# One transformer layer on one core: a unit's weight sums placed between its remainders on VectorE, and raw weight blocks laid side by side

## The chip, the core and the metric

The kernel runs on one core of a Trainium2 chip. The metric is the device time of one execution, in microseconds (us). The core has engines that run beside each other, each with its own queue of instructions in order: TensorE (PE in the profile; PEld is its weight load) multiplies matrices, VectorE (DVE) and ScalarE (ACT) work on elements, GpSimd (POOL) does small work and issues some of the transfers, and SyncE (SP) issues most of them. Transfers between the main memory and the on-chip memory run on 16 DMA engines. Results of TensorE lie in eight banks of accumulators until VectorE or ScalarE reads them. Engines wait for each other through semaphores.

## The reference

One layer over 512 tokens of 2048 features, in float32. Cut to what matters here:

```python
h = rmsnorm(x, norm_mix)
qa, ka, va, qb, kb, vb, ga, gb = split(h @ w_in)
out_a = window_attention(...); out_b = neighbourhood_attention(...)
x = x + (sigmoid(ga) * (out_a @ w_branch_a) + sigmoid(gb) * (out_b @ w_branch_b)) @ w_out
u = rmsnorm(x, norm_ffn) @ w_up                      # 2048 -> 11264
u = centred depthwise convolution of width 3 over the tokens, plus conv_b
gate, val = split(u)
x = x + (silu(gate) * val) @ w_down                  # 5632 -> 2048
```

The gates ga and gb, the up projection and the down projection are the products that the change touches.

## The kernel before

**Float32 by halves.** Each operand of a matmul is split in two: a rounded part, hi (wh for weights), and the remainder, lo (wl). A product is three matmuls: hi by hi, hi by lo, lo by hi. ScalarE rounds (a cast), VectorE subtracts (the remainder).

**Seven products for eight.** Most of the gates and of the two feed-forward projections are computed in 2 x 2 blocks with seven block products where eight would be usual. A `Product` unit is a block of 256 x 512 weights: two blocks of 128 rows (b = 0, 1) by two halves of 256 columns (h = 0, 1). Three of the four raw blocks are used as they are, and four weight forms are sums: with f the unit's tile of seven slices of 128 x 256, `load` (line 588) brings the raw blocks into slices 0, 1, 2 and 6 and `sums` (line 597) makes slices 3 to 6, the first instruction (line 600) two of them at once from the fourth raw block, the second (603) and the third (604) each from the result of the one before. On the activations' side `form_sums` (line 668) does the same kind of work, and `combine` (line 784) puts the seven results of a finished block together in three parts, `one`, `two` and `three`, which read the banks and so free them.

**Units kept.** Some units' weights are made early: `fetch` (line 606) brings the raw blocks by GpSimd's queue, `add` (line 617) makes the sums on VectorE, `store` writes them to main memory (`kept`), in stages where VectorE has room. For such a unit (`made`) `load` brings three raw blocks and the four kept slices, and `sums` does nothing. Of each block of the up projection units 2, 3 and 7 of eight are kept, of the first such block all; of the down projection only a few.

**Forms.** `prep` (line 632) makes the rounded parts and remainders of a unit in two groups: slices 0 to 3 (tag a) and slices 4 to 6 (tag b): a cast on ScalarE (line 645), then a subtraction on VectorE (line 646), for each group. The weight tiles are double buffered by the unit's parity, so a cast waits until TensorE has finished with the unit two before.

**The order.** The loop of `products` (line 690) issues 42 matmuls of a unit (seven forms, two halves of columns, three matmuls each), then calls `advance` (line 179). `advance` first calls `prep` of the unit after next; at the end of a block the parts of `combine` go in as `between`: the first ahead of group a, the second ahead of group b, the third behind. Then it calls `sums` of the unit one further and `load` of the unit two further than that, and last the early work. Behind `advance`, the loop runs one queued piece of work (activation, convolution) and the caller's `after`, which near the changes of stage splits activations that have just been loaded (`split_act`: casts at line 1075, remainders at line 1076). `keep` holds instructions in the order in which the program issues them; the matmuls are placed by the scheduler. The tile f has four buffers, so the load of a unit waits for the remainder of group b four units before; SP issues these loads in order, line 75.

**Stages.** Attention and its projections until about 600 us; gates, branches and w_out to about 1180; the up projection in 22 blocks of eight units to about 2005; then the down projection in three parts of pairs (7, 7 and 8) by four blocks of columns. Three of these twelve blocks (`PLAIN`, the first of part 0 and the last of parts 0 and 1) use plain tiles without sums (`tiles_by_halves`, casts at line 746, remainders at 747). The 195 units that make their sums on the spot are spread over the gates, the up projection and the down projection.

Of the kernel before, what the change touches and what calls it, by code (L numbers as in the profile page):

```python
# [18 lines left out]
P = 128  # L19
# [20 lines left out]
def trunk_kernel(  # L40
# [95 lines left out]
    class Plain:  # L136
# [18 lines left out]
        def prep(self, *between, pieces=1):  # L155
            self.load(pieces)
            for work in between:
                work()
            hi = wst["p"].tile([P, 1024], F32R, tag="hi", name="hi", bufs=2)
            lo = wst["p"].tile([P, 1024], F32R, tag="lo", name="lo", bufs=2)  # L160
            n = 1024 // pieces
            for c in range(0, 1024, n):
                nc.scalar.copy(hi[:, c:c + n], self.raw[:, c:c + n])  # L163
                nc.vector.tensor_tensor(  # L164
                    lo[:, c:c + n], self.raw[:, c:c + n], hi[:, c:c + n].bitcast(F32),
                    ALU.subtract)
            self.hi = hi.rearrange("p (a n) -> p a n", a=self.kpb)
            self.lo = lo.rearrange("p (a n) -> p a n", a=self.kpb)

    def prep_to(n, between=(), **kw):  # L170

        for u in units[at["prep"]:n + 1]:
            if getattr(u, "first", -1) > ffn.get("limit", -1):
                break
            u.prep(*between, **kw)
            between = ()
            at["prep"] += 1
        for work in between:
            work()
# [394 lines left out]
    class Product:  # L574
# [13 lines left out]
        def load(self):  # L588
            f = self.f = ffn["f"].tile([P, 7, 256], F32, tag="f", name="f", bufs=4)
            dma(f[:, 0:2], self.w[:, :, 0])  # L590
            dma(f[:, 2], self.w[:, 1, 1])
            if self.made:
                dma(f[:, 3:], self.kept)
            else:
                dma(f[:, 6], self.w[:, 0, 1])

        def sums(self):
            if not self.made:
                f = self.f
                keep(nc.vector.tensor_tensor(  # L600
                    f[:, 3:5], f[:, 2::-2], f[:, 6].unsqueeze(1).to_broadcast([P, 2, 256]),
                    ALU.add))
                keep(nc.vector.tensor_tensor(f[:, 5], f[:, 4], f[:, 2], ALU.add))  # L603
                keep(nc.vector.tensor_tensor(f[:, 6], f[:, 5], f[:, 1], ALU.add))

        def fetch(self):

            if "q" in ffn:
                x = quad("u").rearrange("p m (t n) -> p (m t) n", t=2)
                self.early = x[:, :2], x[:, 2:]  # L610
            else:
                self.early = [slot().rearrange("p (t n) -> p t n", t=2) for _ in range(2)]
# [19 lines left out]
        def prep(self, *between):  # L632
            self.parts = []
            for b, (tag, n) in enumerate((("a", 4), ("b", 3))):
                if between:
                    between[b]()
# [10 lines left out]
                self.parts += [(hi[:, i], lo[:, i]) for i in range(n)]  # L647
            for work in between[2:]:
                work()
# [72 lines left out]
    class Tiles:  # L722
# [13 lines left out]
        def sums(self):  # L736
            pass

        def prep(self, *between):
# [9 lines left out]
            for work in between:  # L749
                work()  # L750
# [488 lines left out]
```

## Time and profile before

| what | value |
|---|---|
| median of 3 runs | 2465.93 us (2465.27 to 2466.05) |
| profiled execution, from its first instruction to its last | 2464.1 us |
| TensorE busy | 2436.6 us, 99% of the span |
| VectorE busy | 1899.6 us, 77% |
| ScalarE busy | 1283.5 us, 52% |
| moved by DMA | 525.45 MB, 213 GB/s on average |
| mean granted TensorE clock | 0.998 |

The profile is of one execution, and gives its span; the runs' time holds some 1.8 us more, what lies around the span. A busy share is an average over stages: TensorE at 99% can still wait in a stage, and an engine at 77% can be the one that it waits for there. In the lists of instructions, `out<-in` names the tiles that an instruction writes and reads, `xcount` how many there are, and square brackets the idle time of the engine ahead of the instruction and what ended it.

### The profile page before, as it was taken

To read this page: it belongs to the slowest core of one execution; us is meant where nothing else is said; L and a number is where in the kernel's file an instruction comes from. 1 tells how busy PE (TensorE), PEld (TensorE's weight loads), DVE (VectorE), ACT (ScalarE), POOL (GpSimd) and SP (SyncE) were. 2 spreads that over 40 slices of the span, in tenths; PEclk is the share of its full clock that TensorE was granted. 3 is DMA by queue.
4 is the path that set the end of the run, shared out by engine and by line. 5 is a ranking of instruction groups with operands and counts; after the bars stand their busy time and mean duration, and the time that the engine had idled before them with its cause. 6 is when DMAs were issued, how large, how long until landed. Compare 5 with 4: busy or idle time off the path is not lost.

```text
span 2464.1 us, 45745 instructions
## 1 busy us (share of the span) xinstructions
PE 2436.6 (99%) x17430; PEld 2276.2 (92%) x17430; DVE 1899.6 (77%) x3003; ACT 1283.5 (52%) x1962; POOL 330.5 (13%) x406
## 2 busy tenths in 40 slices
PE   9999999999999999999999999999999999999998
PEld 7888888888999888888999999999999999999998
DVE  6787667655888656557888888888888878696898
ACT  5354554365644322334666666666666666453633
POOL 1322122301000111111011111110111101000000
PEclk9999999999999999999999999999999999999999
DMA  5766766746655677777588888888888897766754
GB/s 197 257 230 213 234 207 230 238 139 205 197 163 175 200 271 245 237 232 245 166 213 230 224 225 224 218 234 222 224 228 218 234 277 187 218 187 176 221 158 131
DMA packets 340700, 525.45 MB, mean 213 GB/s; under 512 B 30720, under 2 KB 234112, under 8 KB 340480
## 3 DMA queue, kind: packets, MB, share of 16 engines
q1 hardware_dynamic: 254656, 319.68, 41.8%
q0 software_dynamic: 48384, 128.91, 21.8%
q10 hardware_dynamic: 37440, 73.94, 7.8%
q8 instruction: 136, 2.23, 0.4%
q14 instruction: 84, 0.69, 0.1%
HBM read 377.80 MB, written 98.57 MB: 193 GB/s over the span
## 4 chain that ended last, share of the span: by engine, by line
PE 94%; DVE 2%; DMA 1%; ACT 1%; issue 1%; SPq 0%; DVEq 0%; ACTq 0%
PE mm L78 91%; PE tr L78 2%; PE tr L503 1%; PE tr L351 0%; DVE wl L646 0%; DVE s L1076 0%; DMA a<-in_x_t 0%; DMA s<-act 0%; DMA f<-in_w_down 0%; ACT wh L645 0%; DVE u L795 0%; DVE s L687 0%; ACT s L1075 0%; DMA sums<-s 0%; DVE s L620 0%
## 5 line engine op out<-in xcount | busy, mean ns | idle before, releaser
L78 PE MATMUL mm<-s,wh 128*128 128x256 f32 (+1 forms) x9620 | 1725.0, 289 | 6.6 <-ACT wh L645 2.5
L78 PEld LDWEIGHTS mm<-s,wh 128*128 128x128 f32 x9620 | 1437.1, 188 | 48.7 <-ACT wh L645 3.1
L78 PE MATMUL mm<-s,wl 128*128 128x256 f32 (+1 forms) x4810 | 1249.9, 289 | 3.5 <-DVE wl L646 3.5
L78 PEld LDWEIGHTS mm<-s,wl 128*128 128x128 f32 x4810 | 851.0, 188 | 24.7 <-DVE wl L646 4.5
L645 ACT CAST wh<-f 128x1024 fp32r<-128x1024 f32 (+1 forms) x566 | 516.9, 942 | 482.5 <-PE mm L78 331.3
L646 DVE TENSOR_TENSOR wl<-f,wh 128x1024 fp32r<-128x1024 f32 (+1 forms) x566 | 601.8, 1088 | 147.7 <-ACT wh L645 146.3
L78 PE MATMUL mm<-hi,s 128*128 128x512 f32 x896 | 284.9, 394 | 5.7 <-ACT hi L163 5.7
L747 DVE TENSOR_TENSOR wl<-f,wh 128x1024 fp32r<-128x1024 f32 x85 | 104.1, 1224 | 165.4 <-ACT wh L746 159.7
L746 ACT CAST wh<-f 128x1024 fp32r<-128x1024 f32 x85 | 89.4, 1052 | 238.8 <-PE mm L78 207.0
L78 PEld LDWEIGHTS mm<-hi,s 128*128 128x128 f32 x896 | 167.6, 189 | 38.4 <-ACT hi L163 5.7
L163 ACT CAST hi<-raw 128x1024 fp32r<-128x1024 f32 (+1 forms) x97 | 100.9, 1040 | 188.5 <-PE mm L78 153.9
L78 PE MATMUL mm<-s,hi 128*128 128x512 f32 x640 | 195.4, 392 | 2.1 <-ACT o L519 1.6
L164 DVE TENSOR_TENSOR lo<-raw,hi 128x1024 fp32r<-128x1024 f32 (+1 forms) x97 | 117.5, 1211 | 102.8 <-ACT hi L163 98.7
L78 PE MATMUL mm<-lo,s 128*128 128x512 f32 x448 | 176.3, 395 | 0.0
L78 PEld LDWEIGHTS mm<-s,hi 128*128 128x128 f32 x640 | 119.2, 188 | 25.9 <-ACT o L519 1.8
L600 DVE TENSOR_TENSOR f<-f 128x512 f32<-128x512 f32 x195 | 133.5, 685 | 0.0
L1045 POOL DMA_DIRECT2D o<-a x44 | 52.9, 1202 | 557.8 <-ACT a L1044 336.9
L78 PE MATMUL mm<-s,lo 128*128 128x512 f32 x320 | 118.8, 391 | 0.0
L620 DVE TENSOR_TENSOR s<-s 128x256 f32<-128x256 f32 x236 | 93.2, 419 | 17.1 <-DMA s<-in_w_up 15.0
L78 PEld LDWEIGHTS mm<-lo,s 128*128 128x128 f32 x448 | 84.4, 188 | 16.6
L1042 ACT ACTIVATE o<-u,smalls 128x512 f32<-128x512 f32 x88 | 71.2, 809 | 33.3 <-DVE t L677 30.1
L603 DVE TENSOR_TENSOR f<-f 128x256 f32<-128x256 f32 x195 | 83.0, 426 | 6.7
(150 smaller groups left out, 2029.5 us busy)
## 6 DMA issues: line engine op xcount, KB each, us to landing
f<-sums SPq DMA_DIRECT2D x88, 512.0 KB, 5.3
f<-in_w_up SPq DMA_DIRECT2D x176, 256.0 KB, 3.8
o<-a POOLq DMA_DIRECT2D x88, 511.0 KB, 7.4
f<-in_w_up SPq DMA_DIRECT2D x281, 128.0 KB, 3.8
raw<-in_w_in SPq DMA_DIRECT2D x63, 512.0 KB, 4.4
sums<-s ACTq DMA_DIRECT2D x118, 256.0 KB, 4.1
s<-in_w_up POOLq DMA_DIRECT2D x86, 256.0 KB, 5.4
s<-act SPq DMA_DIRECT2D x168, 128.0 KB, 4.2
```

What stands on the lines that cost most here:

```text
L78: return nc.tensor.matmul(o, l, r, start=start, stop=stop, skip_group_check=True).ins
L163: nc.scalar.copy(hi[:, c:c + n], self.raw[:, c:c + n])
L164: nc.vector.tensor_tensor(lo[:, c:c + n], self.raw[:, c:c + n], hi[:, c:c + n].bitcast(F32), ALU.subtract)
L600: keep(nc.vector.tensor_tensor(f[:, 3:5], f[:, 2::-2], f[:, 6].unsqueeze(1).to_broadcast([P, 2, 256]), ALU.add))
L603: keep(nc.vector.tensor_tensor(f[:, 5], f[:, 4], f[:, 2], ALU.add))
L620: add = lambda *args: keep(nc.vector.tensor_tensor(*args, ALU.add))
L645: keep(nc.scalar.copy(hi, f))
L646: keep(nc.vector.tensor_tensor(lo, f, hi.bitcast(F32), ALU.subtract))
L746: keep(nc.scalar.copy(hi, self.f))
L747: keep(nc.vector.tensor_tensor(lo, self.f, hi.bitcast(F32), ALU.subtract))
L1042: keep(nc.scalar.activation(self.o[:, m], u[:, m], AF.Identity, bias=cb[:, i:i + 1], scale=cw[:, i, 1:2]))
L1045: keep(nc.gpsimd.dma_start(self.o[:, :, 1:], first[:, :, :S - 1], accum_op=ALU.add))
```

## The change

It does three things. The raw blocks get other slices: w[:, 1] (the second block of rows, both halves of columns) goes to slices 0 and 1, w[:, 0] to slices 2 and 3; slice 3 is overwritten by a sum. So a unit with sums has two loads in place of three, and where the two halves of columns adjoin in memory (w_in, w_down) a row of a load is 2 KB in place of 1 KB. `prep` puts the forms back in the old order for the matmuls. `fetch` and `add` follow the same layout.

The three instructions of `sums` become a list. `advance` hands them to `prep` as hooks: the first goes between group a and group b of the unit that is being prepared, behind group a's remainder; the second goes behind group b; the third is carried to the next `advance` and stands ahead of group a there. The parts of `combine` stand in the same three places, each behind the sum that is there. The sums still belong to the unit one further than the one prepared.

```diff
     def advance(*between):
-        prep_to(at["use"] + 1, between)
-        for phase, d in (("sums", 2), ("load", 4)):
+        def phase_units(phase, d):
             while at[phase] < len(products_) and products_[at[phase]].ready(phase, at["use"] + d):
-                getattr(products_[at[phase]], phase)()
                 at[phase] += 1
+                yield products_[at[phase] - 1]
+
+        hooks = [[*carried], [], []]
+        carried.clear()
+        for u in phase_units("sums", 2):
+            run_all(carried)
+            carried.clear()
+            ops = u.sums()
+            for place, op in zip((1, 2), ops):
+                hooks[place].append(op)
+            carried.extend(ops[2:])
+        for place, op in enumerate(between):
+            hooks[place].append(op)
+        prep_to(at["use"] + 1, hooks)
+        for u in phase_units("load", 4):
+            u.load()
         make_early()
...
         def load(self):
             f = self.f = ffn["f"].tile([P, 7, 256], F32, tag="f", name="f", bufs=4)
-            dma(f[:, 0:2], self.w[:, :, 0])
-            dma(f[:, 2], self.w[:, 1, 1])
+            dma(f[:, 0:2], self.w[:, 1])
             if self.made:
+                dma(f[:, 2], self.w[:, 0, 0])
                 dma(f[:, 3:], self.kept)
             else:
-                dma(f[:, 6], self.w[:, 0, 1])
+                dma(f[:, 2:4], self.w[:, 0])
 
         def sums(self):
-            if not self.made:
-                f = self.f
-                keep(nc.vector.tensor_tensor(
-                    f[:, 3:5], f[:, 2::-2], f[:, 6].unsqueeze(1).to_broadcast([P, 2, 256]),
-                    ALU.add))
-                keep(nc.vector.tensor_tensor(f[:, 5], f[:, 4], f[:, 2], ALU.add))
-                keep(nc.vector.tensor_tensor(f[:, 6], f[:, 5], f[:, 1], ALU.add))
+            if self.made:
+                return []
+            f = self.f
+            add = lambda *args: keep(nc.vector.tensor_tensor(*args, ALU.add))
+            return [
+                lambda: add(f[:, 4:2:-1], f[:, 2:0:-1],
+                            f[:, 3].unsqueeze(1).to_broadcast([P, 2, 256])),
+                lambda: add(f[:, 5], f[:, 4], f[:, 1]),
+                lambda: add(f[:, 6], f[:, 5], f[:, 0])]
 
         def fetch(self):
...
-            for h, x in enumerate(self.early):
-                keep(nc.gpsimd.dma_start(x, self.w[:, :, h]))
+            for b, x in enumerate(self.early):
+                keep(nc.gpsimd.dma_start(x, self.w[:, b]))
 
         def add(self):
             a, b = self.early
...
-            add(c[:, 0], b[:, 1], b[:, 0])
-            add(c[:, 1], a[:, 0], b[:, 0])
-            add(b[:, 0], c[:, 1], b[:, 1])
-            add(b[:, 1], b[:, 0], a[:, 1])
-            self.early = c, b
+            add(c[:, 1], a[:, 0], a[:, 1])
+            add(c[:, 0], b[:, 1], a[:, 1])
+            add(a[:, 0], c[:, 1], b[:, 1])
+            add(a[:, 1], a[:, 0], b[:, 0])
+            self.early = c, a
...
-        def prep(self, *between):
-            self.parts = []
+        def prep(self, *hooks):
+            forms = []
             for b, (tag, n) in enumerate((("a", 4), ("b", 3))):
-                if between:
-                    between[b]()
+                run_all(hooks[b])
...
                 f = self.f[:, 4 * b:4 * b + n]
                 keep(nc.scalar.copy(hi, f))
                 keep(nc.vector.tensor_tensor(lo, f, hi.bitcast(F32), ALU.subtract))
-                self.parts += [(hi[:, i], lo[:, i]) for i in range(n)]
-            for work in between[2:]:
-                work()
+                forms += [(hi[:, i], lo[:, i]) for i in range(n)]
+            run_all(*hooks[2:])
+            self.parts = [forms[i] for i in (2, 0, 1, 3, 4, 5, 6)]
```

`run_all` calls the pieces of work in the lists it is given. Plain units and tiles have no sums; they call the hooks as before.

More of the change, by code (lines that the diff above doesn't have):

```diff
@@ L153, in load, with prep @@
                 c0 += n
-        def prep(self, *between, pieces=1):
+        def prep(self, *hooks, pieces=1):
             self.load(pieces)
-            for work in between:
-                work()
+            run_all(*hooks)
             hi = wst["p"].tile([P, 1024], F32R, tag="hi", name="hi", bufs=2)
@@ L168, in prep, with prep_to @@
             self.lo = lo.rearrange("p (a n) -> p a n", a=self.kpb)
-    def prep_to(n, between=(), **kw):
+    def prep_to(n, hooks=((), (), ()), **kw):
         for u in units[at["prep"]:n + 1]:
@@ L174, in prep_to, with run_all @@
                 break
-            u.prep(*between, **kw)
-            between = ()
+            u.prep(*hooks, **kw)
+            hooks = (), (), ()
             at["prep"] += 1
-        for work in between:
-            work()
+        run_all(*hooks)
+    def run_all(*hooks):
+        for works in hooks:
+            for work in works:
+                work()
+    carried = []
     def advance(*between):
-        prep_to(at["use"] + 1, between)
-        for phase, d in (("sums", 2), ("load", 4)):
+        def phase_units(phase, d):
             while at[phase] < len(products_) and products_[at[phase]].ready(phase, at["use"] + d):
-                getattr(products_[at[phase]], phase)()
                 at[phase] += 1
+                yield products_[at[phase] - 1]
[13 more added lines that the diff above has]
+            u.load()
         make_early()
@@ L589, in load @@
             f = self.f = ffn["f"].tile([P, 7, 256], F32, tag="f", name="f", bufs=4)
-            dma(f[:, 0:2], self.w[:, :, 0])
-            dma(f[:, 2], self.w[:, 1, 1])
+            dma(f[:, 0:2], self.w[:, 1])
             if self.made:
+                dma(f[:, 2], self.w[:, 0, 0])
                 dma(f[:, 3:], self.kept)
             else:
-                dma(f[:, 6], self.w[:, 0, 1])
+                dma(f[:, 2:4], self.w[:, 0])
         def sums(self):
-            if not self.made:
-                f = self.f
-                keep(nc.vector.tensor_tensor(
-                    f[:, 3:5], f[:, 2::-2], f[:, 6].unsqueeze(1).to_broadcast([P, 2, 256]),
-                    ALU.add))
-                keep(nc.vector.tensor_tensor(f[:, 5], f[:, 4], f[:, 2], ALU.add))
-                keep(nc.vector.tensor_tensor(f[:, 6], f[:, 5], f[:, 1], ALU.add))
+            if self.made:
[7 more added lines that the diff above has]
+                lambda: add(f[:, 6], f[:, 5], f[:, 0])]
         def fetch(self):
             if "q" in ffn:
-                x = quad("u").rearrange("p m (t n) -> p (m t) n", t=2)
-                self.early = x[:, :2], x[:, 2:]
-            else:
-                self.early = [slot().rearrange("p (t n) -> p t n", t=2) for _ in range(2)]
-            for h, x in enumerate(self.early):
-                keep(nc.gpsimd.dma_start(x, self.w[:, :, h]))
+                x = quad("u").rearrange("p b (h n) -> p b h n", h=2)
+                self.early = x[:, 0], x[:, 1]
+            else:
+                self.early = [slot().rearrange("p (h n) -> p h n", h=2) for _ in range(2)]
+            for b, x in enumerate(self.early):
+                keep(nc.gpsimd.dma_start(x, self.w[:, b]))
         def add(self):
@@ L646, in prep @@
                 keep(nc.vector.tensor_tensor(lo, f, hi.bitcast(F32), ALU.subtract))
-                self.parts += [(hi[:, i], lo[:, i]) for i in range(n)]
-            for work in between[2:]:
-                work()
+                forms += [(hi[:, i], lo[:, i]) for i in range(n)]
+            run_all(*hooks[2:])
+            self.parts = [forms[i] for i in (2, 0, 1, 3, 4, 5, 6)]
     def make_early():
@@ L736, in sums, with prep @@
         def sums(self):
-            pass
-        def prep(self, *between):
+            return []
+        def prep(self, *hooks):
             hi, lo = (
@@ L748, in prep @@
             self.hi, self.lo = (v.rearrange("p (b c) n -> p b (c n)", b=2) for v in (hi, lo))
-            for work in between:
-                work()
+            run_all(*hooks)
     class TilesByHalves(Tiles):
```

## The prediction

> **What bounds the kernel now.** I read the page first, then the chain that ended last in order of time, then the busy time by stretches, and last each place where TensorE sat idle.
>
> ```profile
> span 2464.1 us, 45745 instructions
> ...
> PE 2436.6 (99%) x17430; PEld 2276.2 (92%) x17430; DVE 1899.6 (77%) x3003; ACT 1283.5 (52%) x1962; POOL 330.5 (13%) x406
> ```
> ```profile
> 636.33 547.52 PE mm L78 x3286
> ...
> 1202.54 802.51 PE mm L78 x7058
> ```
> TensorE is the bound. From 636 to 2005 us the chain is matmul after matmul, so whatever VectorE or the queues do there is hidden. Most of the changed instructions run there and can earn nothing. Only a stretch in which TensorE waits can pay. The next view has the end of the kernel, the down projection; behind the stretch and its length stand the busy time and the matmuls started on PE, then PEld, DVE, ACT, POOL, the clock, the DMA share and GB/s.
>
> ```profile
> 2004.00:2016.00 12.00, 8.47 (x53) 7.47 (x52) 7.21 (x14) 9.22 (x22) 1.20 (x1) 0.85 1.08 293
> 2016.00:2164.00 148.00, 147.45 (x1281) 146.93 (x1280) 116.44 (x196) 81.75 (x152) 10.00 (x10) 0.99 0.76 216
> 2164.00:2182.00 18.00, 16.85 (x146) 16.52 (x145) 17.51 (x38) 11.66 (x25) 1.72 (x2) 1.00 0.87 229
> 2182.00:2295.00 113.00, 113.00 (x996) 113.00 (x995) 86.87 (x131) 48.32 (x71) 5.16 (x6) 1.00 0.65 181
> 2295.00:2352.00 57.00, 53.41 (x462) 52.62 (x461) 54.04 (x97) 31.85 (x62) 3.93 (x6) 1.00 0.66 187
> ```
> The undisturbed row gives the pace: 996 matmuls in 113 us, 8.81 per us. At that pace 18 us hold 158.7 and 57 us hold 502.4. With 146 and 462 started, the third row lost 12.7 / 8.81 = 1.4 us and the fifth 40.4 / 8.81 = **4.6 us**; in both VectorE is busy 95 to 97%. The first row lost 52.7 / 8.81 = 6.0 us, but VectorE is busy for only 7.2 of 12 us there. The stalls one by one (idle time and its releaser in brackets):
>
> ```profile
> 2181.27 0.39 PE L78 MATMUL mm<-s,wl 128*128 128x256 f32 x1 [1.15 <-DVE wl L646]
> ...
> 2320.69 0.39 PE L78 MATMUL mm<-s,wl 128*128 128x256 f32 x1 [0.60 <-DVE wl L646]
> ...
> 2326.56 0.39 PE L78 MATMUL mm<-s,wl 128*128 128x256 f32 x1 [0.82 <-DVE wl L646]
> ...
> 2345.02 0.38 PE L78 MATMUL mm<-s,wl 128*128 128x256 f32 x1 [0.92 <-DVE wl L646]
> ...
> 2351.60 1.09 PE L78 MATMUL mm<-s,wh 128*128 128x256 f32 x7 [1.25 <-ACT wh L645]
> ```
> Four wait for a remainder (wl, line 646), the fifth for a cast (wh, line 645). They sum to 4.74 us; the count of matmuls says 6.0, since TensorE also restarts slowly. This 6.0 us is what the change can win. What else TensorE idles lies ahead of 636 us, in the stages of the attention, and of the changed code only the fetches and adds run there.
>
> **The sums on VectorE.** One unit with weight sums, in the stretch where line 1076 splits activations too:
>
> ```profile
> 2313.54 2.09 DVE L646 TENSOR_TENSOR wl<-f,wh 128x1024 fp32r<-128x1024 f32 x2
> 2315.54 0.69 DVE L600 TENSOR_TENSOR f<-f 128x512 f32<-128x512 f32 x1
> 2316.27 0.43 DVE L603 TENSOR_TENSOR f<-f 128x256 f32<-128x256 f32 x1
> 2316.73 0.43 DVE L604 TENSOR_TENSOR f<-f 128x256 f32<-128x256 f32 x1
> 2317.07 2.43 DVE L1076 TENSOR_TENSOR s<-s 128x256 fp32r<-128x256 f32 x7
> 2319.42 2.09 DVE L646 TENSOR_TENSOR wl<-f,wh 128x1024 fp32r<-128x1024 f32 x2
> ```
> ```profile
> 2340.62 0.68 DVE L795 TENSOR_TENSOR u<-mm,t 128x512 f32<-128x512 f32 x1
> 2341.22 0.68 DVE L795 TENSOR_TENSOR u<-mm,o 128x512 f32<-128x512 f32 x1
> ```
> The three sums read each other's results, and start 0.73, 0.46 and 0.34 us ahead of the next instruction. Instructions that do not depend on each other overlap: line 795 starts again after 0.60 us at the same 512 elements, and seven splits of 256 take 2.35 us, 0.34 each. So the dependence costs 0.13 + 0.12 = **0.25 us a unit**. The change puts a remainder between the first sum and the second, and carries the third into the next call. Where splits stand between the second and third, all 0.25 us goes; where nothing does, only 0.13. The numbers of instructions and elements stay.
>
> The Trainium skill, "VectorE: DVE Perf Modes", section "The DRAIN you can't avoid", says that the next operation does not start until the pipe is empty, and that chaining without semaphores measured the same time. By it, reordering saves nothing here, and the sum is that of the second rival below. The rows above differ: a sum that needs the one before starts after it ends, a split before the last one ends.
>
> **The cast that waits for a sum.** Behind the splits VectorE catches up:
>
> ```profile
> 2353.59 0.69 DVE L600 TENSOR_TENSOR f<-f 128x512 f32<-128x512 f32 x1
> ...
> 2355.44 2.09 DVE L646 TENSOR_TENSOR wl<-f,wh 128x1024 fp32r<-128x1024 f32 x2 [0.24 <-ACT wh L645]
> 2357.45 0.69 DVE L600 TENSOR_TENSOR f<-f 128x512 f32<-128x512 f32 x1
> ```
> ```profile
> 2354.36 1.79 ACT L645 CAST wh<-f 128x1024 fp32r<-128x1024 f32 x2 [2.07 <-DVE f L600]
> ```
> ScalarE's cast of the first group reads the first sum's result, so it starts when that sum ends (2354.28), and VectorE then waits for it. A unit takes 3.86 us. After the change the first sum stands ahead of the second remainder, most of a unit earlier, and that wait goes: 2.01 (the pair) + 0.60 + 0.46 + 0.34 = 3.41 us, so 0.45 us a unit goes here.
>
> ```profile
> 2308.79 0.96 DVE L646 TENSOR_TENSOR wl<-f,wh 128x768 fp32r<-128x768 f32 x1 [0.83 <-ACT wh L645]
> ...
> 2349.67 0.69 DVE L600 TENSOR_TENSOR f<-f 128x512 f32<-128x512 f32 x1
> ```
> At 2308.79 VectorE idles 0.83 us ahead of a second remainder; the first sum of the next unit, 0.60 us, fits in there.
>
> Against the stalls: in the stretch to 2182 three units save 0.75, and VectorE's idle time there, 18 - 17.51 = 0.49, can go: 1.24 against the stall of 1.15, so I take the whole 1.4. From 2295 units with splits follow each other every 5.88 us (2313.54 to 2319.42). By 2320, four of them and the filled idle make 4 x 0.25 + 0.60 = 1.6, against 0.60; by 2326, 1.85 against 0.60 + 0.82 = 1.42; by 2345, three catch-up units more make 1.85 + 3 x 0.45 = 3.2, against 2.34. The fifth stall stands behind the first sum at 2349.67, itself behind the combination of a finished block; that sum now comes ahead of the block's second part. There VectorE is the limit: 3.2 won and its own idle, some 3.8 of the 4.6. Sum: 1.4 + 3.8 = **5.2 us**.
>
> What is delayed: the second remainder by 0.60 us (the first sum ahead of it), and the combination's middle part, which frees banks, by as much at block ends. Both have a unit's time, 42 matmuls / 8.81 = 4.8 us, except at the ends of blocks; that is why I take 3.8 and not 4.6. A new wait: the cast of the second group needs the third sum, which now follows the splits.
>
> ```profile
> 2307.93 0.83 ACT L645 CAST wh<-f 128x768 fp32r<-128x768 f32 x1 [1.76 <-issue]
> 2308.67 0.71 ACT L1075 CAST s<-s 128x256 fp32r<-128x256 f32 x2
> ```
> Behind that cast on ScalarE stand the casts for the next splits (line 1075), and VectorE's splits wait for those. From the third sum's end VectorE has two remainders, 2.01, and two sums, 0.60 + 0.34, to do first; ScalarE is through the cast and two split casts in 0.83 + 0.71 = 1.54. So I take nothing, and as the other end 0.5 us for each unit with sums and splits, of which the timeline shows four up to 2181 and six from 2295.
>
> **The loads.**
>
> ```profile
> L600 DVE TENSOR_TENSOR f<-f 128x512 f32<-128x512 f32 x195 | 133.5, 685 | 0.0
> ```
> ```profile
> SPq L75 <- DVE wl L646: 844.2, 267, 23.6
> ```
> ```profile
> 2361.50 0.89 SPq L75 DMA_DIRECT2D f<-in_w_down x2
> ```
> The 195 units with sums need two loads where they had three; 0.45 us of SP's time goes with each. SP waits 844 us for remainders to free its buffers, which hides it, so I cost it at nothing, up to 0.45 us where SP is late. Longer rows change the matrices whose blocks adjoin, not the up projection's, which lie apart. Line 600 never waited for a load (0.0 idle), and a load is issued some three units before its sum, so moving that sum up by one remainder adds no wait; without this cover VectorE would stand still, with the remainder, the combination and the splits behind.
>
> ```profile
> DVE s L620 <- DMA s<-in_w_up: 15.0, 9, 3.5
> ```
> ```profile
> 475.00:500.00 25.00, 23.76 (x121) 19.93 (x120) 17.58 (x42) 9.96 (x22) 4.76 (x9) 1.00 0.61 218
> ```
> The sums made early (fetch and add) keep their counts; the first add now needs the first of the two loads, not the second. At nine waits and one add of 0.34 us that is at most 3 us of VectorE's, and TensorE idles but 1.24 us of the 25 around some of them; I take nothing.
>
> **The rivals.**
>
> Second: **only the wait for the cast goes**, because dependent sums cost the same wherever they stand. Then the 0.49 of idle wins 0.4 of the first 1.4, and 0.60 at 2308, 3 x 0.24 and 1.2 of the fifth stall win 2.5 of the second: 2.9 us, 2463.0. For it: in catch-up the second and third sum stay adjacent. Against: the overlap in the rows above.
>
> Third: **the new wait takes it back.** 10 x 0.5 = 5.0 us of VectorE's time against 5.2 won, 2465.7. For it: ScalarE runs one call ahead of VectorE in the splits, and loses that. Against: it is busy for only 11.66 of 18 and 31.85 of 57 us.
>
> Fourth: **the change of stage at 2005 mends too.**
>
> ```profile
> 1995.39 0.40 SPq L75 DMA_DIRECT2D f<-in_w_down  x1
> ```
> ```profile
> 2004.78 1.05 ACT L746 CAST wh<-f 128x1024 fp32r<-128x1024 f32 x1 [4.64 <-DMA f<-in_w_down]
> ```
> ```profile
> 2010.00:2015.00 5.00, 3.11 (x17) 2.92 (x18) 2.59 (x4) 3.50 (x8) 0.00 (x0) 0.74 1.07 264
> 2015.00:2020.00 5.00, 5.00 (x28) 5.00 (x28) 4.69 (x10) 1.45 (x5) 0.00 (x0) 0.58 0.82 272
> ```
> The first tile of w_down is issued at 1995.39 and its cast starts at 2004.78, the DMA engines full (1.07), then the clock falls to 0.58. An earlier load could keep the clock: 28 matmuls instead of 44 in the last row are 1.8 us, and part of the gap before 1 to 2 more: 3 us beside the 5.2, 2457.7. Against: those loads keep their size and order.
>
> Fifth, **slower**: the first sum now writes its two blocks in descending order. Before, it read them so, at 685 ns, and a read cost nothing; such a write the trace does not show. Bounds: nothing, or a second pass, 0.69 us. I take nothing, by the row of the descending read. Above 0.25 us it eats the gain of a unit with splits; at 0.69 the ten such units lose 10 x (0.69 - 0.25) = 4.4 us, and three catch-up units 3 x (0.69 - 0.45) = 0.7, on top of today's stalls: 2471.0.
>
> **How the numbers follow.** The profiled execution spans 2464.1 us, 1.8 less than the median of the runs, 2465.93; I take the 5.2 us off the median: **2460.7**. Chances: this forecast 0.44 (2459.2 to 2462.4), the second 0.22, the third 0.13, the fourth 0.10, the fifth 0.11. A measurement tells 0.2% from no change, 4.9 us, so faster means below 2461.0. Some 0.28 of my forecast's 0.44 lies there, its lower part, and with the fourth that is faster 0.38; the rest of it, the second and the third make same 0.51; slower 0.11. The range is 2457.0 to 2467.5: it leaves out the fifth case and the ends of the others.
>
> **What would show it.** Right: the five stalls gone or under 1 us in sum; the catch-up unit at 3.4 us instead of 3.86; line 645's cast no longer behind a sum; the matmuls of the two stretches near 158 and 500. Wrong: a first sum above 0.69 us (fifth); idle time ahead of line 1076 (third); sums as far apart as before (second); a changed gap at 2005 (fourth); new idle on PE at block ends (the delayed bank reads).

## The result and the profile after

| | before | after |
|---|---|---|
| median of 6 runs each | 2465.99 us (2464.67 to 2467.52) | 2472.66 us (2469.93 to 2475.33) |
| span of the profiled execution | 2464.1 us | 2473.6 us |
| first attention's last output copied at | 353.3 us | 359.4 us |
| second attention's last output copied at | 578.6 us | 585.2 us |
| first cast of a product's weights at | 623.7 us | 634.9 us |
| row factors for the up projection at | 1183.7 us | 1196.0 us |

The changed kernel is slower: ratio 1.0025 [1.0014, 1.0037], 6.7 us, where 5.2 us less was forecast. The table locates it. The profiled execution of after is the slowest of its six (2475.33 us), so its marks are some 2.7 us later in all than a median run's. After is 6.1 us late when the first attention ends, 6.6 at the end of the second, 11.2 at the first product and 12.3 at the row factors; it ends 9.5 us late, so behind the row factors it wins 2.8 us. The gain is where it was forecast. The loss lies in the attention, in which of the changed code only the early fetches and adds run, and at the start of the products.

Two things make up the loss. Up to the row factors TensorE idles 12.3 us in after and 5.9 in before (counted from 20 us on). And its granted clock is at 0.50 in three spells of after, at 264, 585 and 636 us, and in before in none between 9 and 2012 us. In these spells TensorE is busy for 12.5 us, at half speed, which takes some 6.3 us by this working. Together with the 6.4 us of idle time that is the 12.3 us, within 0.4. All six runs of after have a mean clock of 0.995 or 0.996; the runs of before that were timed beside the experiments have 0.997 to 1.000.

**The loss, in the first attention.** Each kernel's VectorE timeline (start, length, line, operation; in brackets the idle time ahead of it and what ended it), before first:

```profile
257.60 0.53 DVE L508 TENSOR_TENSOR pl<-tr,ph 128x384 fp32r<-128x384 f32 x1
258.04 0.42 DVE L620 TENSOR_TENSOR s<-s 128x256 f32<-128x256 f32 x1
261.92 0.76 DVE L620 TENSOR_TENSOR s<-s 128x256 f32<-128x256 f32 x2 [3.46 <-DMA s<-in_w_up]
262.60 1.22 DVE L164 TENSOR_TENSOR lo<-raw,hi 128x1024 fp32r<-128x1024 f32 x1
```

and after:

```profile
258.95 0.89 DVE L642 TENSOR_TENSOR s<-s 128x256 f32<-128x256 f32 x2
259.75 0.16 DVE L509 TENSOR_TENSOR sm<-sm,es 128x4 f32<-128x4 f32 x1
262.75 0.76 DVE L642 TENSOR_TENSOR s<-s 128x256 f32<-128x256 f32 x2 [2.84 <-DMA s<-in_w_up]
263.43 0.55 DVE L527 TENSOR_TENSOR pl<-tr,ph 128x384 fp32r<-128x384 f32 x1
...
281.89 0.43 DVE L642 TENSOR_TENSOR s<-s 128x256 f32<-128x256 f32 x1 [4.74 <-DMA s<-in_w_up]
```

In both kernels an early add waits for its load with VectorE's queue behind it. Before, the attention's remainder `pl` stands ahead of the waiting add; after, it stands behind one. TensorE after:

```profile
264.03 0.46 PE L78 MATMUL tr<-pl,s 128*128 128x384 f32 x1 [2.43 <-DVE pl L527]
...
285.53 0.50 PE L78 MATMUL mm<-lo,s 128*128 128x512 f32 x1 [1.42 <-DVE lo L163]
```

It waits 2.43 us for that remainder and 1.42 us for one behind the add of 281.89. The granted clock (third figure from the end) falls behind the first of these waits, by the windows of after, PE's busy time and matmuls standing before it:

```profile
262.00:264.00 2.00, 0.00 (x0) 1.00 1.01 388
264.00:266.00 2.00, 1.97 (x7) 0.58 0.95 376
266.00:268.00 2.00, 2.00 (x7) 0.56 0.68 233
268.00:270.00 2.00, 2.00 (x11) 1.00 0.40 98
```

A window counts every matmul that runs in it, so one that lies across the end of a window counts in both neighbours. From 255 to 290 us, as one window, before has 176 matmuls and after 146. At before's 176 / 35 = 5.0 per us the 30 are 6.0 us: 3.85 of waits, 1.7 by the slow clock (3.4 us at half), and a rest of 0.4. This is the 6.1 us of the table. What VectorE waits in all for early loads tells nothing of it, 23.6 us before and 20.7 after:

```profile
DVE s L620 <- DMA s<-in_w_up: 15.0, 9, 3.5
DVE o L620 <- DMA u<-in_w_up: 8.6, 3, 4.1
```
```profile
DVE s L642 <- DMA s<-in_w_up: 13.1, 8, 4.7
DVE o L642 <- DMA u<-in_w_up: 7.6, 6, 2.7
```

**The loss, at the first product.** ScalarE's timeline, before and then after:

```profile
623.72 1.77 ACT L645 CAST wh<-f 128x1024 fp32r<-128x1024 f32 x2
625.39 1.33 ACT L872 ACTIVATE a<-a,gmix 128x512 f32<-128x512 f32 x2
```
```profile
632.05 1.34 ACT L892 ACTIVATE a<-a,gmix 128x512 f32<-128x512 f32 x2 [2.61 <-DMA a<-in_x_t]
633.29 1.65 ACT L869 ACTIVATE o<-o 128x512 f32<-128x512 f32 x3
634.85 1.76 ACT L666 CAST wh<-f 128x1024 fp32r<-128x1024 f32 x2
```

After, the product's first cast stands behind an activation that waits 2.61 us for a load of x; before, it stands ahead of one. TensorE, before and then after, waits for that cast:

```profile
624.80 1.91 PE L78 MATMUL mm<-s,wh 128*128 128x256 f32 x14 [1.27 <-ACT wh L645]
```
```profile
635.93 2.37 PE L78 MATMUL mm<-s,wh 128*128 128x256 f32 x11 [3.18 <-ACT wh L666]
```

That is 1.9 us more. Most of the rest of what is lost between the second attention and the row factors is the clock, by these windows of after (the last is before at the same place):

```profile
581.80:585.20 3.40, 1.84 (x10) 1.00 0.38 154
585.20:592.00 6.80, 5.71 (x13) 0.50 0.55 182
636.40:639.80 3.40, 3.40 (x18) 0.50 0.63 200
```
```profile
578.60:585.40 6.80, 5.68 (x25) 1.00 0.80 236
```

From 585 to 592 us after runs 13 matmuls where before, as idle in 6.8 us, runs 25. In the window ahead TensorE is idle for 1.56 us of 3.40, in two waits of 0.59 and 0.95 us, and a stall of 1.11 us follows.

**The gain, in the down projection.** The timeline of after, TensorE's stalls, and VectorE in a unit with splits, then ScalarE, then VectorE in catch-up:

```profile
2193.54 0.95 PE L78 MATMUL mm<-s,wh 128*128 128x256 f32 x6 [0.90 <-ACT wh L666]
...
2332.47 0.96 PE L78 MATMUL mm<-s,wh 128*128 128x256 f32 x6 [0.32 <-ACT wh L666]
...
2338.09 0.97 PE L78 MATMUL mm<-s,wh 128*128 128x256 f32 x6 [0.58 <-ACT wh L666]
```
```profile
2326.91 0.68 DVE L621 TENSOR_TENSOR f<-f 128x512 f32<-128x512 f32 x1
2327.51 0.95 DVE L667 TENSOR_TENSOR wl<-f,wh 128x768 fp32r<-128x768 f32 x1
2328.38 0.41 DVE L621 TENSOR_TENSOR f<-f 128x256 f32<-128x256 f32 x1
2328.71 2.42 DVE L1096 TENSOR_TENSOR s<-s 128x256 fp32r<-128x256 f32 x7
2331.06 0.41 DVE L621 TENSOR_TENSOR f<-f 128x256 f32<-128x256 f32 x1
2331.40 1.21 DVE L667 TENSOR_TENSOR wl<-f,wh 128x1024 fp32r<-128x1024 f32 x1
2332.53 0.68 DVE L621 TENSOR_TENSOR f<-f 128x512 f32<-128x512 f32 x1
```
```profile
2331.59 0.83 ACT L666 CAST wh<-f 128x768 fp32r<-128x768 f32 x1 [1.68 <-DVE f L621]
```
```profile
2362.08 0.68 DVE L621 TENSOR_TENSOR f<-f 128x512 f32<-128x512 f32 x1
2362.69 0.95 DVE L667 TENSOR_TENSOR wl<-f,wh 128x768 fp32r<-128x768 f32 x1
2363.55 0.88 DVE L621 TENSOR_TENSOR f<-f 128x256 f32<-128x256 f32 x2
...
2365.48 0.69 DVE L621 TENSOR_TENSOR f<-f 128x512 f32<-128x512 f32 x1
```

And the windows that answer to the two stretches that lost (some 12 us later):

```profile
2176.00:2194.00 18.00, 17.05 (x147) 16.66 (x146) 17.30 (x39) 13.32 (x30) 1.72 (x2) 1.00 0.87 228
...
2307.00:2364.00 57.00, 56.10 (x491) 55.70 (x490) 55.18 (x101) 34.73 (x64) 3.92 (x6) 1.00 0.67 197
```

No stall for a remainder is left in the two stretches. The long one holds 491 matmuls instead of 462: 29 / 8.81 = 3.3 us. The short one holds 147 instead of 146. Matched matmul by matmul, after is 12.4 us late at 640 us of before, 12.3 at 2004, 12.9 at 2182, 12.7 at 2295 and 9.5 at 2352: the units up to 2004 us win and lose nothing, the change of stage at 2005 loses some 0.6 to 0.7, and the long stretch wins 3.2 to 3.3. The three stalls that are there, 1.8 us in sum, are new: a cast that waits for the third sum, which stands behind the splits.

### The profile page after: what moved, and what is told of

Read it like the earlier page. It is cut to its first block, busy times and chain, and to the rows that moved or that the text cites. A ratio compares the mean times of both kernels' runs of the same rounds, so it can differ in the third digit from the quotient of the medians.

```text
span 2473.6 us, 45487 instructions
## 1 busy us (share of the span) xinstructions
PE 2442.7 (99%) x17430; PEld 2280.3 (92%) x17430; DVE 1870.4 (76%) x3003; ACT 1288.5 (52%) x1962; POOL 332.0 (13%) x406
## 4 chain that ended last, share of the span: by engine, by line
PE 71%; DMA 2%; DVE 1%; ACT 0%; issue 0%; SPq 0%; DVEq 0%; ACTq 0%
PE mm L78 71%; DMA s<-act 1%; DVE s L1096 1%; DMA f<-in_w_down 0%; DVE f L621 0%; ACT wh L666 0%; DVE u L815 0%; DVE wl L667 0%; SPq L75 0%; ACT s L1095 0%; DVE t L815 0%; PE mm L295 0%; PE mm L284 0%; DVE t L837 0%; DVEq L1255 0%
## 5 line engine op out<-in xcount | busy, mean ns | idle before, releaser
L78 PE MATMUL mm<-s,wh 128*128 128x256 f32 (+1 forms) x9620 | 1742.7, 289 | 9.1 <-ACT wh L666 5.0
L78 PEld LDWEIGHTS mm<-s,wh 128*128 128x128 f32 x9620 | 1456.3, 188 | 52.5 <-ACT wh L666 6.0
L78 PE MATMUL mm<-s,wl 128*128 128x256 f32 (+1 forms) x4810 | 1289.3, 289 | 0.0
L78 PEld LDWEIGHTS mm<-s,wl 128*128 128x128 f32 x4810 | 869.0, 188 | 19.9
L666 ACT CAST wh<-f 128x1024 fp32r<-128x1024 f32 (+1 forms) x566 | 524.8, 942 | 483.1 <-PE mm L78 357.8
L667 DVE TENSOR_TENSOR wl<-f,wh 128x1024 fp32r<-128x1024 f32 (+1 forms) x566 | 612.6, 1088 | 176.8 <-ACT wh L666 170.4
L621 DVE TENSOR_TENSOR f<-f 128x256 f32<-128x256 f32 (+1 forms) x585 | 297.5, 509 | 5.6 <-DMA f<-in_w_down 0.9
L1065 POOL DMA_DIRECT2D o<-a x44 | 52.9, 1202 | 574.6 <-ACT a L1064 436.6
L1073 POOL DMA_DIRECT2D o<-a x44 | 52.8, 1201 | 187.4 <-ACT a L1071 139.0
```

Of the source, the lines that this page charges most:

```text
L78: return nc.tensor.matmul(o, l, r, start=start, stop=stop, skip_group_check=True).ins
L621: add = lambda *args: keep(nc.vector.tensor_tensor(*args, ALU.add))
L666: keep(nc.scalar.copy(hi, f))
L667: keep(nc.vector.tensor_tensor(lo, f, hi.bitcast(F32), ALU.subtract))
L1065: keep(nc.gpsimd.dma_start(self.o[:, :, 1:], first[:, :, :S - 1], accum_op=ALU.add))
L1073: keep(nc.gpsimd.dma_start(self.o[:, :, :S - 1], third[:, :, 1:], accum_op=ALU.add))
```

## The experiments

Why would the attention's order change, when its code did not? The scheduler places the attention's instructions around the early adds. In before the first add needs the second of a unit's two loads, in after the first. In the order of instructions of the two compiled programs, the first one on VectorE that has another place is an early add (at 102 us; in before a reduction stands in that place). Theory one: the place of these adds costs the time. Its rivals are named with each run. Where an expectation speaks of the start of the products, it means TensorE's first matmul of them, at 624.8 us in before and 635.9 in after; the text gives the first cast, some 1.1 us ahead of that. The matmul counts of 416 and 430 for 2300 to 2350 us in the expectations are sums of two windows of 25 us; as one window, before holds 414. All times are medians; before was run beside each, at 2465.41 (experiments one to four), 2465.98 (five to eight) and 2465.5 (nine to eleven).

**One: the changed kernel, the first two early adds swapped**, so that the first needs both loads.

```diff
-            add(c[:, 1], a[:, 0], a[:, 1])
             add(c[:, 0], b[:, 1], a[:, 1])
+            add(c[:, 1], a[:, 0], a[:, 1])
```

> The changed kernel with its first two early adds in the other order, so that the first one needs both loads again, as before the change. Everything else of the change stays: layout, longer rows, sums between the remainders. Theory (the order of these two adds sets the program's order in the attention, and the loss is there): the attention runs as before, the products start near 625 us as before (936 ns steps of the profile aside: 624.8 against 635.9 in the changed kernel), and the end gains the 2.8 us that the changed kernel gained behind 1196 us: about 2463, ratio 0.998 to 1.000. Rival 1 (the longer rows of the early loads, or their layout, cost the attention): products start near 636, about 2472, ratio 1.0025. Rival 2 (the sums between the remainders cost something that the attention only hides): between the two, 2467 or more with the products starting at 625.

2465.1 us, ratio 0.9999 [0.999, 1.0008]. Two swapped lines take back the whole loss. VectorE and TensorE have before's order again up to the products, the first cast comes at 625.9 us, and the gain behind it is there (2350 to 2375 us: 223 matmuls, before 210). The time is 2 us above the theory's 2463, and these 2 us are missing between before's 623.7 and 625.9. (No view here shows the steps of 936 ns that the expectation sets aside.)

**Two: before with only the changed fetch and add.**

```diff
-            for h, x in enumerate(self.early):
-                keep(nc.gpsimd.dma_start(x, self.w[:, :, h]))
+            for b, x in enumerate(self.early):
+                keep(nc.gpsimd.dma_start(x, self.w[:, b]))
...
-            add(c[:, 0], b[:, 1], b[:, 0])
+            add(c[:, 1], a[:, 0], a[:, 1])
...
```

> The kernel before with nothing but the changed fetch and add. Loads, sums and prep are those of before. Theory: the attention is that of the changed kernel, the rest that of before: the products start 8 to 12 us late, near 635, and the end stays as before: 2472 to 2478, ratio 1.003 to 1.005. Rival (the loss comes from the sums or the loads of the units): the time of before, 2466.

2475.62 us, 1.0042 [1.003, 1.0055]. The early part alone has the whole loss: first attention to 360.1 us, first cast at 635.8. Up to the products its order on VectorE and TensorE is that of after, and its clock has four spells at 0.50 (285, 531, 589 and 637 us).

**Three: the new layout everywhere, the early adds swapped as in one, the sums together as before.**

```diff
-            dma(f[:, 0:2], self.w[:, :, 0])
-            dma(f[:, 2], self.w[:, 1, 1])
+            dma(f[:, 0:2], self.w[:, 1])
...
+            add(f[:, 5], f[:, 4], f[:, 1])
+            add(f[:, 6], f[:, 5], f[:, 0])
```

> The new layout everywhere with its longer rows and two loads for three, the early adds in the swapped order, and the three sums together behind both remainders, as before the change. Theory: nothing of the loads is on the path, 2466 within 1 us, ratio 0.9995 to 1.0005, and the down projection's five stalls are there as before, some 4.7 us of idle time on TensorE. Rival (the fewer and longer loads give part of what the changed kernel gained at the end): 2464 or less. Rival (the descending write of the first sum costs): line of the first sum above 700 ns and 2468 or more.

2468.09 us, 1.0011 [1.0003, 1.002], first cast at 625.4. This misses the theory's 2466 by more than its 1 us, and neither rival is it: the time is not 2464, and the first sum lasts 683 ns. The layout wins nothing; the late start of one is here too.

**Four: the changed kernel, each early add two units behind its loads.**

```diff
-        if fetched and u - fetched[0][1] >= 1 + wide:
+        if fetched and u - fetched[0][1] >= 2:
```

> The changed kernel, but in the attention the early adds are made two units after their loads in place of one, so that their data has landed when VectorE comes to them. Theory (the first adds stand in VectorE's queue ahead of their data and hold up the attention behind them): VectorE's waits for loads in these adds fall from 13 us to under 4, and the attention loses less: products start before 632, 2464 to 2469. Rival (it is the order itself, not the waits for data): still 2470 or more with the waits gone. Open: two more tiles are held, so a tile may come free too late and the loads start later, which would show as GpSimd waiting.

2464.48 us, 0.9995 [0.9986, 1.0004]. VectorE's waits for early loads fall from 20.7 to 4.7 us (4.3 and 0.4), and the first attention ends at 354.3 instead of 359.4. GpSimd waits longer for the adds to free their tiles, as the expectation left open (80.2 us instead of 41.4), and the attention is shorter all the same. But TensorE then waits 4.1 us for the first product's cast, again behind an activation that waits for a load of x (2.79 us), with a spell at half clock of 3.4 us behind it. The order on the engines is another one again, so the run doesn't tell the waits from the order.

**Five: the sums' place alone, in before.** Loads, layout and early sums stay.

```diff
-        prep_to(at["use"] + 1, between)
+        hooks = [[*carried], [], []]
...
+        prep_to(at["use"] + 1, hooks)
```

> Only the place of the three sums is changed; loads, their layout and the early sums are those of before, and all engines keep before's order up to the products. Theory one (what the sums' place gains behind 1196 us is real, and the 2 us by which products start late in the first and third experiment come from the longer rows or the earlier loads): products start at 624.8 +- 0.5 us as before, 2300 to 2350 us holds 430 matmuls or more instead of 416, and the time is 2.5 to 3.7 us under before: 2461.7 to 2463.0. Rival (the late start is nothing of the rows, and comes and goes with any compile): products start at 626 to 627 here too, and the time is within 1 us of before, about 2465.

2462.69 us, 0.9986 [0.9977, 0.9995]: 3.3 us faster. First cast at 624.1; 2300 to 2350 us holds 428 matmuls instead of 414. Theory one holds: the idea of the change works alone, and the late start is not the sums'.

**Six: before, the early loads in longer rows, adds swapped**, which has before's order on every engine, instruction by instruction (waits aside). The adds also write and store other tiles than in before.

```diff
-            for h, x in enumerate(self.early):
-                keep(nc.gpsimd.dma_start(x, self.w[:, :, h]))
+            for b, x in enumerate(self.early):
+                keep(nc.gpsimd.dma_start(x, self.w[:, b]))
...
+            add(c[:, 0], b[:, 1], a[:, 1])
+            add(c[:, 1], a[:, 0], a[:, 1])
```

> Before, with the early units' two loads in longer rows and the first two early adds swapped, so that every engine's order is that of before, instruction by instruction. Theory one (the order alone costs the 9 to 10 us; longer rows of the early loads cost nothing): 2465.4 +- 1, products from 624.8 +- 0.5. Rival a (the longer rows of these early loads delay the x loads beside them): products from 626 to 627, 2467 to 2468. Rival b (longer rows themselves cost what the second experiment lost): 2474 or more.

2467.62 us, 1.0009 [1.0001, 1.0018], first cast at 625.3: near rival a. The late start comes with this early part. GpSimd's and ScalarE's timelines of before and then of this kernel have the difference in one load of x:

```profile
609.12 0.72 POOL L865 DMA_DIRECT2D a<-in_x_t  x1 [5.21 <-ACT s L686]
610.40 1.34 ACT L872 ACTIVATE a<-a,gmix 128x512 f32<-128x512 f32 x2 [1.39 <-DMA a<-in_x_t]
```
```profile
609.93 1.34 ACT L872 ACTIVATE a<-a,gmix 128x512 f32<-128x512 f32 x2 [0.50 <-DMA a<-in_x_t]
610.96 0.72 POOL L865 DMA_DIRECT2D a<-in_x_t  x1 [7.41 <-DVE s L687]
```

ScalarE's row tells when the load of x issued before this one has landed: at 610.4 and 609.9 us. In before the load is issued ahead of that landing. Here it is issued behind it: in GpSimd's queue the wait for that landing stands ahead of the load, where before has it behind. The same holds for the other kernels with before's order in the attention: one and three, which start late, issue this load behind the landing; five, seven and eleven, which don't, ahead of it. So rival a has its time and its start right, but the rows show a wait in another place and not a slower transfer; the last early load ahead of it was issued at 481 us. What moves the wait, the rows or the tiles that the adds write, no run tells.

Rival b falls: rows as long as in experiment two cost 1.6 us here and 10.2 there.

**Seven: before with the new layout and longer rows of a unit's own tile only.**

```diff
-                dma(f[:, 6], self.w[:, 0, 1])
+                dma(f[:, 2:4], self.w[:, 0])
```

> Before, with the unit's f tile loaded in the new layout by longer rows (two loads for three where not early), the sums together as before, the early units' loads and adds as before. Theory one (the late start comes with the early loads): products from 624.8 +- 0.5, 2465.4 +- 1. Rival a (it comes with the longer rows of f): products from 626 to 627, 2467 to 2468. Rival b (the descending write of the first sum costs over 0.05 us): the first sum lasts over 0.60 us and the time is 2468 or more at a start of 624.8.

2466.87 us, 1.0001 [0.9992, 1.001], first cast at 623.8. Two loads for three are worth nothing. Rival b is out: the first sum lasts 684 ns, and before's lasts 685 (the 0.60 us of the expectation is the distance to the next instruction, not the length).

**Eight: the sums' place as in five, adds later as in four, before's loads.**

```diff
-        if fetched and u - fetched[0][1] >= 1 + wide:
+        if fetched and u - fetched[0][1] >= 2:
```

> The sums' place alone as in the fifth experiment, with before's loads, and each early add two units behind its loads instead of one (while the loads are narrow). Theory one (early adds that wait for loads at the head of VectorE's queue cost attention nothing in before, 23.6 us of such waits, but would if others queue behind): VectorE's waits of the early adds for loads fall from 23.6 us to under 5, and the time is that of the fifth experiment less what the late start of the fourth (2 us or so) takes, 2461 to 2465. Rival (the first order is a matter of luck between the engines and any move of the early adds may cost several us): products start at 630 or later, and the time is 2468 or more.

2465.12 us, 0.9995 [0.9986, 1.0003], with the first cast at 629.3 and the start of the products on TensorE at 630.4. Neither side is right in full. VectorE's waits for early loads fall from 23.6 to 11.8 us and not under 5, and the time is just above the 2461 to 2465 of theory one; the start has the rival's sign (630 or later), but the time is far under its 2468. The profiled execution is the slowest of the eleven (2469.21 us), so the late start may not be that of a median run. By the medians later adds cost 2.4 us against five: to move the adds is no cure by itself.

**Nine: the changed kernel, its early adds reading a constant.**

```diff
-            add(c[:, 1], a[:, 0], a[:, 1])
-            add(c[:, 0], b[:, 1], a[:, 1])
-            add(a[:, 0], c[:, 1], b[:, 1])
-            add(a[:, 1], a[:, 0], b[:, 0])
+            d = c.rearrange("p t (k n) -> p t k n", k=2)
+            o = ones.unsqueeze(1).to_broadcast([P, 2, P])
+            add(d[:, 1], o, o)
+            add(d[:, 0], o, o)
+            add(d[:, 1], d[:, 1], o)
+            add(d[:, 0], d[:, 0], o)
```

> The changed kernel, whose early adds read a constant tile in place of the loaded blocks: as many adds of the same size at VectorE, and the same loads and stores, but no add waits for a load. The early sums are left out by this, so the output is another. Theory one (attention loses because remainders stand behind adds that wait for their loads): VectorE's waits of early adds for loads fall from 20.7 us to under 2, the eighth output copy of the second attention comes by 580 us instead of 585.2, the first product's cast by 628 us instead of 634.9, and the time is 2461 to 2467. Rival (the order of the other instructions, which the compiler places anew, is what costs, whether an add waits or not): the cast comes at 633 us or later, and the time is 2470 or more.

2459.94 us, 0.9976 [0.9967, 0.9985], under the 2461 to 2467 of theory one. This kernel leaves out the early sums and serves to measure alone. It has as many adds and loads, and no wait between them: the first attention ends at 349.6 us, the second's last copy comes at 557.3, the first cast at 623.7. (The lead of 21 us at the second attention's end is gone at the first cast: between kernels of different orders that mark compares little.) Its windows on TensorE (busy, matmuls, clock, DMA share, GB/s) show the stretch in which after has 104 and 117 matmuls:

```profile
250.00:275.00 25.00, 25.00 (x126) 1.00 0.94 328
275.00:300.00 25.00, 25.00 (x132) 1.00 0.38 125
```

The order of this kernel is neither before's nor after's, so a new order need not cost anything. That after's adds cost by their waits fits this run, but the run doesn't isolate it, since the order is not after's.

**Ten: before, a unit's two early loads issued the other way round.**

```diff
-            for h, x in enumerate(self.early):
-                keep(nc.gpsimd.dma_start(x, self.w[:, :, h]))
+            for h in (1, 0):
+                keep(nc.gpsimd.dma_start(self.early[h], self.w[:, :, h]))
```

> Before, with the two early loads of a unit issued the other way round, and nothing else: rows, tiles and adds are those of before, but the first add now has its data with the first load instead of the second. Theory one (what the change loses is that the first add is placed a load earlier than the rest of the unit's data allows): the first product's cast comes at 629 us or later, and the time is 2469 to 2475, with rows that are not longer. Rival (the loss needs the longer rows): cast by 626, time 2465 to 2467.

2474.34 us, 1.0032 [1.002, 1.0045]: with before's rows and adds, 8.8 us are lost because the first add has its data with the first load. The rival falls. But the loss lies elsewhere. The first attention is faster than before's (350.1 us), and VectorE waits only 8.6 us for early loads. It is lost from the second attention on:

```profile
507.88 2.11 PE L78 MATMUL mm<-s,hi 128*128 128x512 f32 x8 [1.44 <-ACT hi L163]
...
524.39 0.63 PE L78 MATMUL tr<-s 128*128 128x256 f32 x2 [1.01 <-ACT s L239]
...
632.17 3.36 PE L78 MATMUL mm<-s,wh 128*128 128x256 f32 x14 [3.09 <-ACT wh L645]
```

The last of these is after's second loss (after waits 3.18 us there, before 1.27). The clock is at 0.50 in three spells, at 526, 584 and 631 us, the last of them:

```profile
631.50:638.30 6.80, 6.13 (x28) 0.50 0.72 243
```

Up to the row factors this kernel is 9.9 us late: TensorE idles 9.3 us instead of 5.9, and the three spells, 12.9 us of work at half speed, take some 6.5. So the adds' waits do not explain all: the order that follows from the early placing costs in a second place too, and there mostly by the clock.

**Eleven: the changed kernel with before's fetch and add.**

```diff
-                x = quad("u").rearrange("p b (h n) -> p b h n", h=2)
-                self.early = x[:, 0], x[:, 1]
+                x = quad("u").rearrange("p m (t n) -> p (m t) n", t=2)
+                self.early = x[:, :2], x[:, 2:]
...
```

> The changed kernel with before's early loads and adds: the sums stand between the remainders, and a unit's own blocks lie in the new layout and come in the longer rows. Theory one (the two parts outside the early sums are worth what they were alone: -3.3 us and +0.9 or nothing): cast of the first product at 624 us, 2300 to 2350 us with 430 matmuls or more, time 2461.7 to 2464. Rival (the two loads for three meet the interleaved sums' earlier need and give part back): 2465 or more.

2462.91 us, 0.9986 [0.9977, 0.9995], first cast at 623.3, 429 matmuls from 2300 to 2350. With five, this is the version that beats both kernels.

The parts, by the medians: the sums' place -3.3 us, the unit's layout +0.9 or nothing, the early part's rows and tiles +1.6 to +2.3 (six; eleven against one; seven against three), the first add's need 7.0 (after against one) to 8.6 (two against six). They sum to between 5.3 and 8.5; measured were 6.7.

## Why the prediction was wrong

**The step that failed** is in the paragraph on the loads: "the first add now needs the first of the two loads, not the second ... at most 3 us of VectorE's, and TensorE idles but 1.24 us of the 25 around some of them; I take nothing." It priced an instruction that may start earlier in an order that stays. The order did not stay: the attention's instructions are placed around the add by the scheduler, and an earlier add put a remainder behind a wait for a load. In place of nothing, the first add's need cost 7.0 us (after against one) to 8.6 (two against six). For the sum at line 600 the prediction named what would stand still behind a wait; for the adds it did not. TensorE's idle time in the same windows of before is no bound either, since it shows only what stood behind the adds there. Nor had any term of the sum the clock, which takes about half of what after loses up to the row factors (6.3 of 12.3 us). No rival had this case, the fifth ended slower for another reason.

**Point by point:**
- Only stretches in which TensorE waits can pay: held. From the row factors on, after wins 2.8 us, and five and eleven 3.3 and 2.6 in the whole.
- The dependence between sums costs 0.25 us a unit: held. Units with splits follow each other after 2332.53 - 2326.91 = 5.62 us, before 5.88. The first sum is followed after 0.60 us where it was 0.73. So the second rival is out. The Trainium skill, "VectorE: DVE Perf Modes", section "The DRAIN you can't avoid", as the prediction read it, would have had 5.88 again; the trace does not agree with that reading. The section also says that a next operation that is not held starts earlier, which the prediction left out, and the 0.60 us agree with that.
- The catch-up unit at 3.41 us: measured 2365.48 - 2362.08 = 3.40, before 3.86.
- The new wait of a cast for the third sum, taken as nothing: mis-sized. ScalarE idles 1.68 us ahead of that cast, and TensorE 0.90, 0.32 and 0.58, 1.8 us in three places. The third rival had the wait of the cast, at 5.0 us, but not what stands behind it: its sign, idle time of VectorE ahead of the splits, is not there, and TensorE waits for the cast itself. For it the two stretches won 0.1 + 3.3 = 3.4 us, where 1.4 + 3.8 = 5.2 were forecast.
- The first sum's descending write, nothing: held (684 ns); the fifth rival is out.
- Two loads for three, nothing: held (seven). The first sum, moved up, waits for a load once in 195 times, 0.9 us.
- The change of stage at 2005, the fourth rival: not mended; from 2004 to 2016 us eleven holds 48 matmuls, before 53, and after loses some 0.6 to 0.7 us there.
- The second remainder and the combination later by 0.60 us, nothing: no stall of TensorE's stands at a block's end in after's list.

**What stays open:** how much of the loss in the attention comes from adds that wait and how much from the order alone, since no run has after's order without the waits; why the clock falls in the order of after, two and ten and not in before's, where waits as long stand (1.63 us at 579.7 us in before, with no spell); and what moves the wait in GpSimd's queue that has the x load of 609 us issued 2 us later. The late first cast of after and ten has a load of x ahead of it, but no run took that load away alone.

## What to carry to other kernels

An instruction whose operands come sooner is not free in a program that a scheduler orders: look at what the new order queues behind it, engine by engine, before it is priced at nothing. Count waits by what stands behind them and not by their sum: with 23.6 us of VectorE's waits TensorE idles 0.5 us in the first attention of before, with 20.7 us in other places 4.8 in that of after. Look at the clock of each stretch as well as at the stalls: here it took about as much as they did. When a change has parts, build each alone; here one part was worth 3.3 us and another hid it.

## What the hardware showed that was not expected

- **A short wait can cost twice.** Behind the stall of 2.43 us in after the clock was at 0.50 for 3.4 us, and 10 matmuls ran in that time where the rate before was 5.0 per us. From 585 to 592 us, beside a stall of 1.11 us, it was at 0.50 again. The length of one stall does not decide: behind that of 1.42 us at 285 us in after and of 1.63 us at 579.7 us in before the clock stayed at 1.00. The Trainium skill, "TensorE: Matmul & The Clock Gate", part 1, has the clock halved after an idle window of some 3.4 us; here shorter stalls were enough, and TensorE was busy for 1.84 of the 3.40 us ahead of the spell at 585 us.
- **A load can be late by the place of a wait.** With the same order of instructions, one load of x on GpSimd's queue was issued at 610.96 instead of 609.12 us, behind the landing of the load before it instead of ahead of it, and the first product's cast came 1.6 us later. Three kernels with the late load and four without it agree (experiment six); no run shows what moves the wait.
- **A tile written in descending blocks costs nothing**: 684 ns at 128 x 512, as ascending (685).
